# One 512-column product for the high weight part in the feed-forwards of a two-block transformer

## The chip, the cores and the metric

The kernel runs on one core of a Trainium2 chip. The metric is the device time of one execution in microseconds (us). Before the change it is 1501.49 us, the median of three runs (1499.78 to 1502.46).

The engines are named as in the profile: PE (TensorE, matrix products), PEld (its weight loads), DVE (VectorE), ACT (ScalarE), POOL (GpSimd) and SP (SyncE, which issues the DMAs here).

## The reference

The input is 256 tokens of 1024 features. A first transformer block has sliding-window and differential attention, then cross attention, then a feed-forward. A second part follows with two layers; each has a feed-forward, a mixer (convolution with latent attention in layer 0, sparse attention in layer 1) and another feed-forward. Nine modulation rows per layer come from a product of a vector `c` with a wide matrix. The parts that the change touches:

```python
u = rms_norm(x, g_mlp[l]) @ w_up[l]                  # first block, 1024 -> 4096
x = x + jnp.square(jax.nn.relu(u)) @ w_down[l]

def swiglu(h, w13, w2):                              # second part, 1024 -> 2 x 2816
    a, b = jnp.split(h @ w13, 2, axis=-1)
    return (jax.nn.silu(a) * b) @ w2

mod = c_act @ ada_w[l] + ada_b[l]                    # nine rows of 1024
h = modulate(x, norm_g[l, 0], sh1, sc1)
x = x + 0.5 * g1[:, None] * swiglu(h, ff_w13[l, 0], ff_w2[l, 0])
```

## The kernel before, in words

Activations lie transposed: features on the 128 partitions, the 256 tokens along the free axis. Every float32 operand of a weight product is used in two parts, a rounded high part and the rest as a low part, and a product is the sum of three: high weight by high activation, high weight by low activation, low weight by high activation (`mm3`). Each of the three takes a 128x128 weight tile as the stationary operand and streams 256 columns.

Weights arrive by DMA in units of 1 MB (16 tiles) into four buffers `raw`. For each half unit (8 tiles, called a split) ACT copies `raw` into the rounded `whi`, and DVE forms `wlo` as `raw` minus `whi` (line 404). `pump` keeps these splits up to three steps of 8 tiles ahead of the products; the low part is issued one split behind the high part.

The order on every engine is the order in which the Python code issues it; there is no scheduler. `run` walks a list of steps. For a step of 8 tiles it first calls `pump`, then issues what was deferred (the splitting of a feed-forward's results into `gh` and `gl`), then the products, and if these end a pair of column tiles, the code that takes the results out of PSUM (`evac`).

- `pairs` makes the steps of `w_up` (16 pairs, 8 row tiles deep) and of `w13` (four feed-forwards of 22 pairs, 8 deep). The first two or three pairs of a `w13` run before the norm is known and go another way (`head`). A pair takes 16 tiles and one PSUM tile of 512 columns, 256 for each column tile.
- `singles` makes the steps of `w_down` (8 column tiles, 32 deep) and of `w2` (8 column tiles, 22 deep). Each result is added to the residual `x` on DVE (lines 1259, 1261), and `norm_part` takes the next norm's sums.
- For `w_up` the results go through DVE (relu and scaling, line 1344) and ACT (square). For `w13`, ACT takes the silu of the first half from PSUM and DVE multiplies by the second half from PSUM (line 1398).
- `with_ada` puts the products for the modulation rows between the steps, from 98 us to about 1100 us: ACT scales a piece of `raw` by the vector and POOL adds it to a sum (line 726). Once two rows are summed, a few products on PE bring them into place.

The feed-forwards of the second part are called (layer, number): (0,0), (0,1), (1,0), (1,1). Their matrices are `w13_00` to `w13_11` and `w2_00` to `w2_11`. Products are all issued at line 345 and activations at line 318, which are helpers.

Of the kernel before, what the change touches and what calls it, by code (L numbers as in the profile page):

```python
# [41 lines left out]
GP = 64  # L42
# [32 lines left out]
def pack_cols(w):  # L75
    """column tiles one after the other, k inside"""
# [4 lines left out]
def early_order(K, M):  # L81
    """(column tile, row tile) in turn: the first half of the rows for the first half of the columns comes first"""
# [12 lines left out]
def pack_rows(w, kk):  # L95
    """kk row tiles a unit, all columns of each"""
# [5 lines left out]
def pack_ada(w):  # L102
    """for each modulation row, units of two row tiles"""
# [154 lines left out]
def merge(a, b):  # L258
    """two lists of steps, each in its order, spread evenly over one another"""
# [11 lines left out]
def rounds(n, *stages, lags=(0, 1, 3, 5)):  # L271
    """the stages of n items, each stage so many rounds behind the first; later stages first in a round"""
# [9 lines left out]
class Kernel:  # L282
    def __init__(self, tc, ctx, dram, out):
# [18 lines left out]
    def t(self, name, shape=None, dt=F):  # L302
        """short-lived"""
# [16 lines left out]
    def table(self, func):  # L320
        """loads the table of a function ahead of its use"""
# [4 lines left out]
    def copy(self, out, in_):  # L326
        """PSUM -> SBUF on whichever of the two engines had less"""
# [11 lines left out]

    def split(self, hi, lo, src):  # L340
# [6 lines left out]
    def mm3(self, out, w, x, start, stop, swap=False):  # L347
        """float32 product of operands in two parts; w stationary unless swap"""
        (wh, wl), (xh, xl) = w, x
        prod = [(wh, xh), (wh, xl), (wl, xh)]  # L350
        if swap:
            prod = [(xh, wh), (xh, wl), (xl, wh)]
        for n, (l, r) in enumerate(prod):
# [59 lines left out]
    def second(self):  # L413
        """the low part of the last split, one split behind its high part"""
# [35 lines left out]
    # ---- products with weights  # L450
    def pairs(self, name, x, kc, evac, unit0=0, npairs=None, st=None, head=0, tags=("mm", "mm"),
              biased=None):
        """steps: column tiles in pairs, k outside; evac(pair, psum [P, 2, S]); the first head pairs are of
        activations not yet normed (their norm's state in st), with the shift in two columns behind them"""
# [23 lines left out]
        for s0 in range(0, total, sub_tiles):  # L478
            def fn(hi, lo, s0=s0):
                for t in range(s0, min(s0 + sub_tiles, total)):  # L480
# [4 lines left out]
                    xh, xl = x[0](k), x[1](k)  # L485
                    fl = dict(start=k == 0, stop=k == kc - 1)
                    if pr < head:
# [3 lines left out]
                        xs = self.h[0][:, k, :]  # L491
# [1335 lines left out]
```

## Time and profile before

| what | value |
|---|---|
| median of three runs | 1501.49 us |
| span of the profiled execution, from the first to the last instruction | 1497.7 us |
| median less span (what lies around it) | 3.8 us |
| mean granted TensorE clock | 0.994 |
| PE busy | 1454.4 us, 97% |
| DVE busy | 1056.4 us, 71% |
| ACT busy | 918.8 us, 61% |
| POOL busy | 635.8 us, 42% |
| DMA moved | 312 MB, 208 GB/s on average |

The profile has no time of its own for the profiled execution besides the span. Products overlap in the records (each is shown for some 280 ns while a new one starts every 120 ns), so a busy PE is read by the distance between starts and not by the length of one product. The other three engines start an operation some 0.1 us before the one before it has ended; here too the distance between starts is what counts.

### The profile page before, as it was taken

The page shows a single profiled execution, that of the slowest core. Times are in us where ns is not written, and L with a number is a line of the kernel's source. Part 1 is how long each engine was busy: PE and PEld are TensorE (multiplying, and loading weights), DVE is VectorE, ACT ScalarE, POOL GpSimd, SP SyncE. Part 2 cuts the span into 40 slices and gives each one's busy share as a digit, 9 for nine tenths or more (in the row PEclk, how much of TensorE's full clock was granted, in tenths as well). Part 3 has the DMA queues.
Part 4 walks back from the last instruction along what each step waited for, and adds up shares of the span by engine and source line. Part 5 has one row for each costly group of instructions (what it writes and reads, how often), then busy time and mean ns, then how long its engine had stood idle before and what let it go on. Part 6 is the DMA issues. An engine that isn't in the chain of part 4 may idle for free.

```text
span 1497.7 us, 28352 instructions
## 1 busy us (share of the span) xinstructions
PE 1454.4 (97%) x11478; PEld 1384.8 (92%) x11478; DVE 1056.4 (71%) x1643; ACT 918.8 (61%) x1666; POOL 635.8 (42%) x466
## 2 busy tenths in 40 slices
PE   8998999999999999998999999999999999999997
PEld 8887989999989989997899999899999877999997
DVE  7967767776658777679887676677665777764553
ACT  6546766777657567664677666576654555654442
POOL 3102433545874567753546659466553200500021
PEclk9999999999999999999999999999999999999999
DMA  8344646677665777654548777577754510355551
GB/s 316 117 141 165 211 159 226 245 268 277 250 253 194 292 255 272 253 195 165 182 172 289 275 277 259 204 274 279 288 215 175 197 57 5 137 197 183 184 174 51
DMA packets 46067, 312.00 MB, mean 208 GB/s; under 512 B 5232, under 2 KB 7024, under 8 KB 9072
## 3 DMA queue, kind: packets, MB, share of 16 engines
q1 hardware_dynamic: 45936, 310.19, 57.7%
q8 instruction: 90, 1.47, 0.4%
q14 instruction: 41, 0.34, 0.1%
HBM read 309.12 MB, written 1.05 MB: 207 GB/s over the span
## 4 chain that ended last, share of the span: by engine, by line
PE 69%; DVE 15%; ACT 7%; DMA 5%; issue 3%; POOL 2%; SPq 0%; POOLq 0%; ACTq 0%; DVEq 0%
PE mm L345 59%; DVE wlo L404 5%; DMA raw<-w 3%; PE o L345 3%; PE sc L345 2%; ACT whi L318 2%; POOL adacc L726 2%; ACT raw L318 1%; PE mmt L345 1%; DVE hlo L653 1%; PE pT L845 1%; DVE hlo L563 1%; PE ada L345 1%; DVE gl L342 1%; DMA raw<-w_up 1%
## 5 line engine op out<-in xcount | busy, mean ns | idle before, releaser
L404 DVE TENSOR_TENSOR wlo<-raw,whi 128x1024 fp32r<-128x1024 f32 (+2 forms) x438 | 625.5, 1434 | 51.0 <-ACT whi L318 50.4
L726 POOL TENSOR_TENSOR adacc<-adacc,raw 128x512 f32<-128x512 f32 x252 | 431.9, 1739 | 415.5 <-ACT raw L318 338.8
L345 PE MATMUL mm<-hlo,whi 128*128 128x256 f32 x1960 | 556.8, 284 | 4.5 <-DVE hlo L653 4.1
L345 PE MATMUL mm<-hhi,whi 128*128 128x256 f32 (+1 forms) x1960 | 558.4, 285 | 1.1 <-ACT whi L318 1.1
L345 PE MATMUL mm<-hhi,wlo 128*128 128x256 f32 (+1 forms) x1960 | 553.4, 282 | 4.6 <-DVE wlo L404 4.6
L318 ACT ACTIVATE whi<-raw 128x1024 fp32r<-128x1024 f32 (+2 forms) x438 | 453.1, 1044 | 112.6 <-DMA raw<-w 75.3
L345 PEld LDWEIGHTS mm<-hlo,whi 128*128 128x128 f32 x1960 | 370.1, 189 | 8.3 <-DVE hlo L653 5.6
L345 PEld LDWEIGHTS mm<-hhi,wlo 128*128 128x128 f32 x1960 | 371.2, 189 | 7.0 <-DVE wlo L404 6.6
L345 PEld LDWEIGHTS mm<-hhi,whi 128*128 128x128 f32 x1960 | 370.3, 189 | 5.1 <-issue 2.5
L345 PE MATMUL mm<-gh,whi 128*128 128x256 f32 x960 | 272.6, 284 | 0.0
L345 PE MATMUL mm<-gh,wlo 128*128 128x256 f32 x960 | 271.6, 283 | 0.0
L345 PE MATMUL mm<-gl,whi 128*128 128x256 f32 x960 | 271.6, 283 | 0.0
L345 PEld LDWEIGHTS mm<-gh,whi 128*128 128x128 f32 x960 | 184.2, 192 | 4.3 <-issue 3.4
L345 PEld LDWEIGHTS mm<-gl,whi 128*128 128x128 f32 x960 | 184.2, 192 | 0.0
L345 PEld LDWEIGHTS mm<-gh,wlo 128*128 128x128 f32 x960 | 184.2, 192 | 0.0
L318 ACT ACTIVATE raw<-raw,sc 128x512 f32<-128x512 f32 x252 | 166.9, 711 | 0.6 <-DMA raw<-ada 0.5
L1398 DVE TENSOR_TENSOR ft<-mm,ft 128x256 f32<-128x256 f32 x79 | 33.4, 423 | 111.6 <-ACT ft L318 111.4
L342 DVE TENSOR_TENSOR gl<-ft,gh 128x256 fp32r<-128x256 f32 x120 | 74.1, 628 | 46.0 <-ACT gh L318 45.8
L569 POOL TENSOR_SCALAR xg<-x,M 128x256 f32<-128x256 f32 x40 | 58.3, 1458 | 98.6 <-DVE x L1261 92.3
L318 ACT ACTIVATE p<-sc,nm 128x128 f32<-128x128 f32 (+1 forms) x120 | 49.9, 421 | 74.1 <-DVE r L829 29.4
L318 ACT ACTIVATE ft<-mm 128x256 f32<-128x256 f32 x79 | 29.8, 378 | 93.5 <-PE mm L345 93.5
L585 POOL TENSOR_TENSOR acc<-acc,sq 128x256 f32<-128x256 f32 x60 | 60.4, 1009 | 44.1 <-ACT sq L318 37.1
(298 smaller groups left out, 1908.4 us busy)
## 6 DMA issues: line engine op xcount, KB each, us to landing
raw<-w SPq DMA_DIRECT2D x132, 1024.0 KB, 4.9
raw<-ada SPq DMA_DIRECT2D x72, 1024.0 KB, 6.2
raw<-w_up SPq DMA_DIRECT2D x16, 1024.0 KB, 5.0
raw<-w_down SPq DMA_DIRECT2D x16, 1024.0 KB, 5.4
raw<-hy_in SPq DMA_DIRECT2D x8, 1024.0 KB, 4.9
raw<-w_in SPq DMA_DIRECT2D x6, 1024.0 KB, 8.0
raw<-nsa_in SPq DMA_DIRECT2D x6, 1024.0 KB, 4.9
raw<-w_ck SPq DMA_DIRECT2D x4, 1024.0 KB, 4.8
```

The costliest lines, as they stand in the source:

```text
L318: return self.nc.scalar.activation(out, in_, func, **k)
L342: self.nc.vector.tensor_tensor(lo, src, hi.bitcast(F), OP.subtract)
L345: self.nc.tensor.matmul(out, lhsT, rhs, start=start, stop=stop, skip_group_check=True)
L404: self.behind = lambda hi=hi[:, :b - a], lo=lo[:, :b - a], src=src: self.nc.vector.tensor_tensor(lo, src, hi.bitcast(F), OP.subtract)
L563: self.deferred.append(lambda: nc.vector.scalar_tensor_tensor(lo, xc, gain(c), hi.bitcast(F), op0=OP.mult, op1=OP.subtract))
L569: nc.gpsimd.tensor_scalar(st["xg", c], xc, gain(c), None, op0=OP.mult)
L585: nc.gpsimd.tensor_tensor(acc, st["acc" + key], sq, OP.add)
L653: nc.vector.scalar_tensor_tensor(*last, op0=OP.add, op1=OP.subtract)
L726: nc.gpsimd.tensor_tensor(half, half, src, OP.add)
L845: self.nc.tensor.transpose(ps[:, s, :], src, self.eye)
L1398: nc.vector.tensor_mul(s, ps[:, 1, :], s)
```

## The change

In `w_up`, `w_down`, `w13` (without its first pairs) and `w2`, a tile's product is issued by the new `mm2`: one product of the high weight part with both parts of the activations, which lie side by side in 512 columns, into a whole PSUM tile of 512 columns; then one product of the low weight part with the high activations, added to the half that holds high by high. The two halves are added when the result leaves PSUM. For `w_up` and `w13` the new `summed` does it: ACT copies the first half to SBUF, DVE adds the second half to it; the silu, the multiplication and the relu then read SBUF. For `w_down` and `w2` the residual is updated twice. A pair of column tiles now takes two PSUM tiles (tags `mm` and `T`) in place of one; the modulation rows' products move from tag `T` to tag `O`. So that both parts lie side by side, `h` becomes one tile of low, high and two shift columns, and the buffers of pool `gp` are made in pairs: 32 of 512 columns in place of 64 of 256. All other products keep three products per tile. The removal of comments is left out below.

```diff
-GP = 64
+GP = 32
...
+    def summed(self, ps):
+        t = self.t("ft")
+        self.act(t, ps[:, 0, :])
+        self.nc.vector.tensor_add(t, ps[:, 1, :], t)
+        return t
...
+    def mm2(self, out, w, x, start, stop):
+        (wh, wl), (xh, _, both) = w, x[:3]
+        self.mm(out.rearrange("p a b -> p (a b)"), wh, both, start=start, stop=False)
+        self.mm(out[:, self.hi_at(x), :], wl, xh, start=False, stop=stop)
...
@@ pairs
-                        if r == 0:
+                        if r == 0 and wide:
+                            state["ps"] = [self.ps("mm", [P, 2, S], "mm"), self.ps("mm", [P, 2, S], "T")]
+                        elif r == 0:
                             state["ps"] = self.ps("mm", [P, 2, S], tags[pr % 2])
-                        self.mm3(state["ps"][:, m, :], w, (xh, xl), start=r == 0, stop=k == kc - 1)
+                        if wide:
+                            self.mm2(state["ps"][m], w, x(k), start=k == 0, stop=k == kc - 1)
+                        else:
+                            self.mm3w(state["ps"][:, m, :], w, (xh, xl), start=r == 0, stop=k == kc - 1)
@@ singles
-                            state[m] = self.ps("mm", [P, S], "S" if early else "mm")
+                            state[m] = self.ps("mm", [P, S], "S") if early else self.ps("mm", [P, 2, S], "mm")
...
+                    if early:
+                        self.mm3w(state[m], w, x(k)[:2], start=first, stop=k == kc - 1)
+                    else:
+                        self.mm2(state[m], w, x(k), start=first, stop=k == kc - 1)
@@ h_part
+        return self.h[:, c, S:2 * S], self.h[:, c, :S], self.h[:, c, :2 * S], None
@@ rows, post of the modulation rows
-                ps = self.ps("ada", [P, 512], "T")
+                ps = self.ps("ada", [P, 512], "O")
...
-                tp = self.ps("adat", [P, 4, P], "T")
+                tp = self.ps("adat", [P, 4, P], "O")
@@ residual
-                if gate is None:
-                    nc.vector.tensor_add(xc, ps, xc)
-                else:
-                    nc.vector.scalar_tensor_tensor(xc, ps, gate(m), xc, op0=OP.mult, op1=OP.add)
+                for part in (ps,) if len(ps.shape) == 2 else (ps[:, 0, :], ps[:, 1, :]):
+                    if gate is None:
+                        nc.vector.tensor_add(xc, part, xc)
+                    else:
+                        nc.vector.scalar_tensor_tensor(xc, part, gate(m), xc, op0=OP.mult, op1=OP.add)
@@ evac_up
-                t = self.t("ft")
-                nc.vector.scalar_tensor_tensor(t, ps[:, m, :], 0.0, stu["rbs"], op0=OP.max, op1=OP.mult)
+                t = self.summed(ps[m])
+                nc.vector.scalar_tensor_tensor(t, t, 0.0, stu["rbs"], op0=OP.max, op1=OP.mult)
                 self.act(t, t, AF.Square)
@@ ff, evac
-                self.act(s, ps[:, 0, :], AF.Silu)
-                nc.vector.tensor_mul(s, ps[:, 1, :], s)
+                s = self.summed(ps[0])
+                self.act(s, s, AF.Silu)
+                nc.vector.tensor_mul(s, self.summed(ps[1]), s)
```

On DVE, in `w13_10`, from one pair of column tiles to the next, before the change. `ft` is the result on its way out of PSUM (`mm`), `gl` its low part, `wlo` the low part of a split.

```order
L1398 TENSOR_TENSOR ft_11949<-mm_11897,ft_11949 128x256
L404 TENSOR_TENSOR wlo_11923<-raw_11656,whi_11922 128x1024
L342 TENSOR_TENSOR gl_11953<-ft_11949,gh_11952 128x256
L404 TENSOR_TENSOR wlo_11955<-raw_11656,whi_11954 128x1024
L1398 TENSOR_TENSOR ft_12018<-mm_11962,ft_12018 128x256
```

The same stretch after the change (`gg` now holds both parts of a result).

```order
L365 TENSOR_TENSOR ft_10637<-mm_10596,ft_10637 128x256
L365 TENSOR_TENSOR ft_10641<-mm_10597,ft_10641 128x256
L1450 TENSOR_TENSOR ft_10637<-ft_10641,ft_10637 128x256
L444 TENSOR_TENSOR wlo_10618<-raw_10432,whi_10617 128x1024
L370 TENSOR_TENSOR gg_10645<-ft_10637,gg_10645 128x256
L444 TENSOR_TENSOR wlo_10653<-raw_10432,whi_10652 128x1024
L365 TENSOR_TENSOR ft_10698<-mm_10660,ft_10698 128x256
```

Where one multiplication from PSUM stood, there are now two additions from PSUM and a multiplication that reads two SBUF tiles.

On ACT, in the same stretch, before the change (`raw` times `sc` is a piece of the modulation rows).

```order
L318 ACTIVATE ft_12018<-mm_11962 128x256
L318 ACTIVATE raw_11697<-raw_11697,sc_707 128x512 x2
L318 ACTIVATE whi_12029<-raw_11785 128x1024
L318 ACTIVATE gh_12021<-ft_12018 128x256
L318 ACTIVATE whi_12062<-raw_11879 128x1024
```

After.

```order
L339 ACTIVATE ft_10637<-mm_10596 128x256
L339 ACTIVATE ft_10637<-ft_10637 128x256
L339 ACTIVATE ft_10641<-mm_10597 128x256
L339 ACTIVATE raw_10346<-raw_10346,sc_683 128x512 x2
L339 ACTIVATE whi_10652<-raw_10432 128x1024
L339 ACTIVATE gg_10645<-ft_10637 128x256
L339 ACTIVATE whi_10678<-raw_10526 128x1024
```

The silu no longer reads PSUM but waits for DVE's first addition, and the second copy out of PSUM stands behind it, ahead of the pieces of the modulation rows and of the next split.

## Rows read from the trace of the kernel before

**Rows 1.** page, first part: span, then busy time, share and instructions of each engine

```profile
span 1497.7 us, 28352 instructions
...
PE 1454.4 (97%) x11478; PEld 1384.8 (92%) x11478; DVE 1056.4 (71%) x1643; ACT 918.8 (61%) x1666; POOL 635.8 (42%) x466
```

**Rows 2.** page, chain that ended last, by engine

```profile
PE 69%; DVE 15%; ACT 7%; DMA 5%; issue 3%; POOL 2%; SPq 0%; POOLq 0%; ACTq 0%; DVEq 0%
```

**Rows 3.** stretches: us, each engine's busy us (instructions), PE clock, DMA share, GB/s

```profile
252.00:346.00 94.00, 92.28 (x754) 88.60 (x753) 69.04 (x99) 70.16 (x128) 42.60 (x28) 1.00 0.71 252
346.00:440.00 94.00, 92.84 (x759) 90.21 (x758) 59.93 (x58) 60.64 (x91) 72.89 (x47) 1.00 0.74 276
480.00:572.00 92.00, 89.74 (x728) 86.47 (x727) 68.35 (x70) 60.47 (x97) 54.48 (x30) 1.00 0.75 272
781.50:842.00 60.50, 60.50 (x509) 60.50 (x508) 42.69 (x43) 43.77 (x70) 39.15 (x22) 1.00 0.79 283
979.00:1076.00 97.00, 97.00 (x812) 96.03 (x812) 69.48 (x72) 68.22 (x109) 59.38 (x33) 1.00 0.78 286
1318.00:1430.00 112.00, 112.00 (x940) 112.00 (x939) 61.92 (x82) 52.88 (x82) 0.00 (x0) 1.00 0.55 189
```

**Rows 4.** waits of PE: us in total, times, longest

```profile
PE mm L345 <- DVE wlo L404: 4.6, 9, 0.9
```

**Rows 5.** timeline of DVE, one pair of w13_11, nothing on POOL

```profile
1385.24 0.42 DVE L1398 TENSOR_TENSOR ft<-mm,ft 128x256 f32<-128x256 f32 x1 [2.71 <-ACT ft L318]
1385.58 1.22 DVE L404 TENSOR_TENSOR wlo<-raw,whi 128x1024 fp32r<-128x1024 f32 x1
1386.71 0.42 DVE L342 TENSOR_TENSOR gl<-ft,gh 128x256 fp32r<-128x256 f32 x1
1387.05 1.22 DVE L404 TENSOR_TENSOR wlo<-raw,whi 128x1024 fp32r<-128x1024 f32 x1
1390.97 0.42 DVE L1398 TENSOR_TENSOR ft<-mm,ft 128x256 f32<-128x256 f32 x1 [2.71 <-ACT ft L318]
```

**Rows 6.** timeline of ACT, the same pair

```profile
1384.82 0.38 ACT L318 ACTIVATE ft<-mm 128x256 f32<-128x256 f32 x1 [3.15 <-PE mm L345]
1385.10 1.05 ACT L318 ACTIVATE whi<-raw 128x1024 fp32r<-128x1024 f32 x1
```

**Rows 7.** pieces of the chain in order: start, us, what

```profile
1312.96 167.39 PE mm L345 x1397
```

**Rows 8.** timeline of PE, 512-column products of w_in_v

```profile
68.99 0.39 PE L345 MATMUL mm<-whi,hlo 128*128 128x512 f32 x1
...
71.09 0.40 PE L345 MATMUL mm<-whi,hlo 128*128 128x512 f32 x1
```

**Rows 9.** timeline of DVE, results of w_up leaving PSUM

```profile
259.07 0.76 DVE L1344 SCALAR_TENSOR_TENSOR ft<-mm,rbs 128x256 f32<-128x256 f32 x2 [2.09 <-PE mm L345]
```

**Rows 10.** timeline of ACT, their squares

```profile
259.52 0.75 ACT L318 ACTIVATE ft<-ft 128x256 f32<-128x256 f32 x2 [1.94 <-DVE ft L1344]
```

**Rows 11.** timeline of DVE, an operation and the next on its result

```profile
720.01 0.42 DVE L1439 TENSOR_TENSOR cvv<-mm,cu 128x256 f32<-128x256 f32 x1 [0.60 <-PE mm L345]
720.47 1.46 DVE L1444 TENSOR_SCALAR ca<-cvv,colp 128x256 f32<-128x256 f32 x1
```

**Rows 12.** DVE line 342: count, shortest, median and longest ns

```profile
L342 DVE TENSOR_TENSOR gl<-ft,gh x120: 410/425/1511, 255.1 to 1426.8; 128x256 fp32r<-128x256 f32 x120
```

**Rows 13.** DVE line 404, the same

```profile
L404 DVE TENSOR_TENSOR wlo<-raw,whi x438: 686/1218/2366, 7.8 to 1480.8; 128x1024 fp32r<-128x1024 f32 x144, 128x608 fp32r<-128x608 f32 x2
```

**Rows 14.** DVE line 1398, the same

```profile
L1398 DVE TENSOR_TENSOR ft<-mm,ft x79: 409/425/428, 470.5 to 1425.4; 128x256 f32<-128x256 f32 x79
```

**Rows 15.** POOL line 726, the same

```profile
L726 POOL TENSOR_TENSOR adacc<-adacc,raw x252: 1266/1499/2354, 124.5 to 1097.5; 128x512 f32<-128x512 f32 x126
```

**Rows 16.** timeline of PE, the last sum of squares

```profile
1489.35 0.61 PE L345 MATMUL ssum<-ones,sq 128*128 128x1 f32 x4 [0.75 <-ACT sq L318]
```

**Rows 17.** groups of ACT: count, busy us, mean ns, idle before and releaser

```profile
L318 ACT ACTIVATE whi<-raw 128x1024 fp32r<-128x1024 f32 x431 | 448.6, 1050 | 112.6 <-DMA raw<-w 75.3 <-DMA raw<-w_down 15.8 <-PE mm L345 8.3
```

More of the change, by code (lines that the diff above doesn't have):

```diff
@@ L292, in __init__, with two @@
         self.flip, self.now = 0, None
+        self.half = {}
         self.deferred, self.behind = [], None
     def g(self, name, dt=F, shape=None):
-        return self.gp.tile(shape or [P, S], dt, name=name, tag="g")
+        key = (name if name in PAIRED else "", dt)
+        t = self.half.pop(key, None)
+        n = 1
+        if t is None:
+            n = 0
+            t = self.half[key] = self.gp.tile([P, 2, S], dt, name=name, tag="g")
+        ap = t[:, n, :]
+        if shape:
+            names = " ".join(f"d{i}" for i in range(len(shape) - 1))
+            ap = ap.rearrange(f"p ({names}) -> p {names}", **{f"d{i}": x for i, x in enumerate(shape[1:])})
+        return ap
+    def two(self, name):
+        if name == "gg":
+            self.half.clear()
+        t = self.gp.tile([P, 2, S], R, name=name, tag="g")
+        return t[:, 0, :], t[:, 1, :], t.rearrange("p a b -> p (a b)")
     def w(self, name, shape, dt=F, tag=None, bufs=2):
@@ L345, in mm, with mm3, mm3w, hi_at @@
         self.nc.tensor.matmul(out, lhsT, rhs, start=start, stop=stop, skip_group_check=True)
-    def mm3(self, out, w, x, start, stop, swap=False):
+    def mm3(self, out, w, x, start, stop):
         (wh, wl), (xh, xl) = w, x
[L350 to L353, printed above, removed]
+        for n, (l, r) in enumerate([(xh, wh), (xh, wl), (xl, wh)]):
             self.mm(out, l, r, start=start and n == 0, stop=stop and n == 2)
+    def mm3w(self, out, w, x, start, stop):
+        (wh, wl), (xh, xl) = w, x
+        for n, (l, r) in enumerate([(wh, xh), (wh, xl), (wl, xh)]):
+            self.mm(out, l, r, start=start and n == 0, stop=stop and n == 2)
+    def mm2(self, out, w, x, start, stop):
+        (wh, wl), (xh, _, both) = w, x[:3]
+        self.mm(out.rearrange("p a b -> p (a b)"), wh, both, start=start, stop=False)
+        self.mm(out[:, self.hi_at(x), :], wl, xh, start=False, stop=stop)
+    def hi_at(self, x):
+        return 1 if len(x) > 3 else 0
     def stream_init(self, steps):
@@ L451, in pairs @@
     def pairs(self, name, x, kc, evac, unit0=0, npairs=None, st=None, head=0, tags=("mm", "mm"),
-              biased=None):
+              biased=None, wide=False):
         steps, state = [], {}
@@ L692, in dst, with h_part @@
             if c == 0:
-                hi = self.work.tile([P, KD, S + 2], R, name="hhi", tag="hhi", bufs=1)
-                lo = self.work.tile([P, KD, S], R, name="hlo", tag="hlo", bufs=1)
-                self.h = (hi, lo)
-            return self.h[0][:, c, :S], self.h[1][:, c, :]
-        return dst
+                self.h = self.work.tile([P, KD, 2 * S + 2], R, name="h", tag="h", bufs=1)
+            return self.h_part(c)
+        return dst
+    def h_part(self, c):
+        return self.h[:, c, S:2 * S], self.h[:, c, :S], self.h[:, c, :2 * S], None
     def h_src(self):
-        return (lambda k: self.h[0][:, k, :S], lambda k: self.h[1][:, k, :])
+        return self.h_part
     def ada_steps(self, l):
@@ L810, in softmax @@
         if roomy:
[L811 removed]
+            p = self.g("p0")[:, :P], self.g("p0")
         else:
@@ L885, in split_out @@
     def split_out(self, ps, name, scale=None):
-        hi, lo = self.g(name + "h", R), self.g(name + "l", R)
+        pair = self.two(name)
+        hi, lo = pair[:2]
         if scale is None:
@@ L891, in split_out @@
             self.nc.vector.scalar_tensor_tensor(lo, ps, scale, hi.bitcast(F), op0=OP.mult, op1=OP.subtract)
-        return hi, lo
+        return pair
     def zeroed(self, name, keep):
@@ L951, in late_loads @@
         nc.sync.dma_start(self.posi[1], self.dram["pos"][:, 1, :])
-        self.mem = [self.g(f"mem{c}") for c in range(KD)]
+        self.mem = [self.g("mem") for c in range(KD)]
         for c in range(KD):
@@ L1053, in mdst @@
         def mdst(c):
-            hm[c] = (self.g(f"hmh{c}", R), self.g(f"hml{c}", R))
+            hm[c] = self.two("hm")
             return hm[c]
@@ L1342, in evac_up @@
             for m in range(2):
-                t = self.t("ft")
-                nc.vector.scalar_tensor_tensor(t, ps[:, m, :], 0.0, stu["rbs"], op0=OP.max, op1=OP.mult)
+                t = self.summed(ps[m])
+                nc.vector.scalar_tensor_tensor(t, t, 0.0, stu["rbs"], op0=OP.max, op1=OP.mult)
                 self.act(t, t, AF.Square)
-                gh, gl = self.g("gh", R), self.g("gl", R)
-                self.deferred.append(lambda gh=gh, gl=gl, t=t: self.split(gh, gl, t))
-                gg[2 * pr + m] = (gh, gl)
-        gsrc = (lambda k: gg[k][0], lambda k: gg[k][1])
+                g = gg[2 * pr + m] = self.two("gg")
+                self.deferred.append(lambda g=g, t=t: self.split(g[0], g[1], t))
+        gsrc = lambda k: gg[k]
         self.gg, self.gsrc = gg, gsrc
-        mlp = self.pairs("w_up", h, KD, evac_up, npairs=16, st=stu)
+        mlp = self.pairs("w_up", h, KD, evac_up, npairs=16, st=stu, wide=True)
         M = self.M[0]
@@ L1448, in evac_z @@
                         nc.vector.tensor_mul(a, src, a)
-                        hi, lo = self.g("yh", R), self.g("yl", R)
-                        self.split(hi, lo, a)
-                        y[c] = (hi, lo)
+                        y[c] = self.two("y")
+                        self.split(y[c][0], y[c][1], a)
         scale = 96 ** -0.5
```

51 lines of the change are left out of this document (25 added, 26 removed).

## The prediction

> **What bounds the kernel now.** I read the busy shares first. PE is busy 97% of the span, DVE 71%, ACT 61% [rows 1]. PE leads the chain of waits too, but only with 69%; DVE has 15% [rows 2]. In all, products wait only 4.6 us for low weight parts, in nine waits [rows 4]. So PE sets the pace, with DVE close behind it in places.
>
> Where, the stretches show [rows 3]. A pair of `w_up` or `w13` takes 16 tiles, 48 products before. I divide a stretch's PE instructions by 48 (a few products for modulation rows make the pair count slightly too high) and get, per pair, time and busy DVE:
>
> - `w_up` (252 to 346): 15.7 pairs, 5.99 us, DVE 4.40.
> - `w13_00` (480 to 572): 15.2 pairs, 6.07 us, DVE 4.51.
> - `w13_01` (781.5 to 842): 10.6 pairs, 5.71 us, DVE 4.03.
> - `w13_10` (979 to 1076): 16.9 pairs, 5.73 us, DVE 4.11.
> - `w13_11` (1318 to 1430): 19.6 pairs, 5.72 us, DVE 3.16.
>
> The last has nothing on POOL, and PE clock is 1.00 (2.4 GHz) in all of them. DVE's extra microsecond in the others comes from POOL. The low weight part takes 1.22 us at the median and up to 2.37 [rows 13], the low part of a result 0.43 and up to 1.51 [rows 12]; both read two SBUF tiles. The multiplication from PSUM never leaves 0.41 to 0.43 [rows 14]. POOL's addition goes the same way, 1.27 to 2.35 us [rows 15].
>
> **The products.** The change takes 2,480 products away: `w_up` 256 tiles, `w_down` 256, `w2` 4 x 176, `w13` 4 x 352 less the 144 tiles of the first nine pairs, one product for each tile. The step of a 256-column product comes from a pair without disturbance: DVE's operations after it start at 1385.24 and 1390.97, 5.73 us or 48 x 119.4 ns [rows 5]; 1,397 products of the last stretch give 119.8 [rows 7]. For 512 columns the trace has the products of `w_in_v`: starts at 68.99 and 71.09, nine steps, 233.3 ns [rows 8]. There the weights stream and the activations are stationary, the other way round than in the new product; I take the same step. A tile falls from 358.2 to 233.3 + 119.4 = 352.7 ns, 5.5 ns less (6.1 by 119.8). All 2,480 tiles together are worth 13.6 us (15.1), and that is the most PE alone can give. A pair goes from 5.73 to 5.64 us.
>
> The Trainium skill (TensorE: Matmul & The Clock Gate, Back-to-back issue gap) gives 131 ns as the sustained spacing of 512-column products in streams with weight loads; by it a tile would save 108 ns. The row above, 233 ns, speaks against it. It is the last rival.
>
> **What leaving PSUM costs.** The change adds 190 copies on ACT (32 in `w_up`, 2 x 79 in `w13`), 190 additions on DVE, and 40 residual updates. They stand in the evacuation of a pair, between the splits that feed PE; behind them on DVE wait the low weight parts, and PE waits for those. For a pair of `w13` I follow DVE from start to start:
>
> - First addition to second: the first result must reach ACT, 0.45 us (259.07 to 259.52) [rows 9, 10]; the silu gives way to the copy after 0.28 (as a copy to a split, 1384.82 to 1385.10 [rows 6]) to 0.37 (half of two squares, 0.75 [rows 10]), I take 0.34; the copy is followed by DVE after 0.42 (1384.82 to 1385.24) [rows 5, 6]. Sum 1.21. DVE stands still for most of it, since nothing else is queued there.
> - Second addition to the multiplication on its result: 0.46 (720.01 to 720.47) [rows 11].
> - Multiplication to the next: 0.34 (1385.24 to 1385.58) [rows 5]. It reads two SBUF tiles now. Beside POOL its like goes from 0.43 up to 1.51 [rows 12]; the extra lies between 0 and, since half of these rows show none, half of 1.1; I take 0.2, towards the median. With the 59 multiplications beside POOL and the 32 rescalings below, the ends move the sum by -18 and +32 us.
>
> That is 2.01 us without POOL and 2.21 with, where before the one multiplication took 0.34: 1.67 and 1.87 more. The other POOL delays I leave as they are, since POOL's work does not change.
>
> On the multiplication, the Trainium skill (SBUF — State Buffer, Who interferes with whom) says that a DVE instruction with two SBUF inputs is shut out by a GpSimd instruction that reads SBUF, while one with a single SBUF input is not. The trace agrees: 428 ns at most from PSUM, 1,511 ns from SBUF. By its full block each of the 91 could wait a whole POOL addition, 1.3 us, and the sum would be some 100 us higher; the median row says that most do not wait at all.
>
> For `w_up`: first addition, rescaling 0.46 later, square 0.45, copy 0.34, second addition 0.42, rescaling 0.46, next 0.34; sum 2.47, with 0.2 for each of two rescalings that now read SBUF 2.87. Before: twice 0.34. So 2.19 more.
>
> DVE then needs, per pair: `w_up` 6.59 us, `w13_00` 6.38, `w13_01` 5.90, `w13_10` 5.98, `w13_11` 4.83. Only the last is below PE's 5.64. In the other four PE must follow DVE.
>
> ACT gets the two short copies, and waits for DVE's addition; its load per pair (68.22 us over 16.9 pairs in `w13_10`, 4.04 us [rows 3]) plus 0.34 and that 0.45 stays below 5.
>
> **The sum**, against the pairs' own times before:
>
> - `w_up` 16 x (6.59 - 5.99) = +9.6
> - `w13_00` 19 x (6.38 - 6.07) = +5.9
> - `w13_01` 20 x (5.90 - 5.71) = +3.8
> - `w13_10` 20 x (5.98 - 5.73) = +5.0
> - `w13_11` 20 x (5.64 - 5.73) = -1.8
> - `w_down` and `w2`: 960 x 5.5 ns = -5.3; DVE has room there for the one more update a column tile (59.93 of 94 us busy in `w_down` [rows 3]).
> - The end: the last residual takes one more update, 0.46, which the last sum of squares waits for (PE already idles 0.75 there [rows 16]); the same at five earlier ends, mostly under the next first pairs: +1.0 in all.
> - Credit for the splits that run ahead: after a pair's end DVE needs about 0.42 + 2.2 + 1.6 us to the next low part that PE lacks, and PE has two more steps, 5.64 us, so each of the four stretches may fall 1.4 us behind at no cost: -5.6.
>
> Total +12.6 us. Span 1497.7 becomes 1510.3; with the 3.8 us between span and median, 1514 us. The measured pair times of DVE vary, so the likeliest case's own range is 1504.5 to 1524.
>
> The modulation rows' move to another PSUM tag, the pairing of buffers and the new layout of `h` I cost at nothing: POOL, SP and the loads keep their order, and the tags have the same number of buffers. Without that cover it is a wait of a few hundred ns at a modulation row or in an attention stage.
>
> **Rivals.**
>
> 1. *The gain of PE comes through* (0.24). DVE's cycle stays under 5.64 us in the busy stretches. For `w13_01` this needs 0.26 us less than I count, for `w13_10` 0.34, and it is a matter of POOL: while DVE stands still between the two additions, POOL can work undisturbed, so part of the microsecond that POOL costs DVE per pair may go. The single point is whether that pays back 0.3 us a pair. Against it: DVE already idles more than a microsecond per pair before, in which POOL had the same freedom. If so, 13.6 less 1.0 for the end: 1489 us.
> 2. *DVE without reserve delays the loads* (0.13). ACT waits 75.3 us in all for `raw` [rows 17], with DMA 71 to 79% busy in these stretches [rows 3]. A buffer is freed by the low part on DVE; a later DVE means a later load, and nothing is left for catching up. Then no credit for running ahead (+5.6), and both middle feed-forwards at the load of `w13_00`, 0.4 us a pair more for 40 pairs (+16): 1535 us.
> 3. *Both sides cancel* (0.11): extra on DVE of only 0.2 us a pair less over 75 pairs, about -12: 1502 us.
> 4. *The wide product is much cheaper than in the row* (0.02). If it took no longer than a narrow one, 119.4 ns, PE would need 3.8 us a pair and DVE would set every pair: +24 in the four stretches, -18 in `w13_11` (4.83), up to -115 in `w_down` and `w2`, +1 at the end: 1394 us. The 512-column rows speak against it.
>
> The Trainium skill's spacing, named above, points to this rival.
>
> That the change does not act as told is excluded: the program has the 2,480 products fewer.
>
> **Numbers.** The forecast has 0.50: 1514 us. Changes below 0.2% (3 us) can't be told from none. Slower by more: the forecast but for its lowest edge (0.47) and rival 2, 0.60. Faster: rivals 1 and 4, 0.26. Within: 0.14. The range reaches from rival 1 to rival 2, 1490 to 1535.
>
> **What would show it.** After the change: `w13_11` near 5.64 us a pair with DVE idle before its first addition; in the other four stretches PE waits for `wlo`, far above 4.6 us in total, pairs of 5.9 us and more, and ACT waiting for DVE's additions. A 512-column step near 233 ns confirms the PE term. If `w13_01` and `w13_10` also run at 5.64 with PE idle nowhere, the DVE sum is wrong and rival 1 holds; if ACT waits much more than 75 us for loads, rival 2.

## The result, and the profile after

The changed kernel takes 1573.34 us (1572.28 to 1575.48, four runs) where the one before, on the same chip, takes 1500.65. The ratio is 1.0481, 95% interval 1.0463 to 1.0499. Slower was forecast, but by 12.6 us; the profiled spans differ by 1571.7 - 1497.7 = 74.0 us, far above the range.

The page of the changed kernel, against [rows 1, 2]: span, busy time of each engine, and the chain that ended last.

```profile
span 1571.7 us, 23765 instructions
...
PE 1465.5 (93%) x8998; PEld 1261.8 (80%) x8998; DVE 1174.8 (75%) x1873; ACT 982.9 (63%) x1856; POOL 631.7 (40%) x466
...
PE 31%; DVE 20%; ACT 7%; DMA 5%; issue 2%; POOL 1%; POOLq 0%; ACTq 0%; SPq 0%; DVEq 0%
```

PE has 2,480 instructions fewer; DVE has more to do. The shares of the chain after the change add up to 66% only, since the profile could follow it back no further than to 521.9 us. Of the part that it has, PE holds 31 of 66, less than half, where before it held 69% of the whole; DVE holds 20 of 66, where it had 15%. The waits of PE for low weight parts and for POOL's sums of the modulation rows (us, times, longest), the first against [rows 4]:

```profile
PE mm L373 <- DVE wlo L444: 53.2, 53, 2.7
PE ada L373 <- POOL adacc L776: 14.6, 13, 2.7
```

PE waited 4.2 us for POOL's sums before. For the stages, two sets of windows, each from the first split of a result to the last one of a stage behind its `head` pairs. Columns as in [rows 3]. First before, 14, 18, 19, 19 and 19 pairs of `w_up`, `w13_00`, `w13_01`, `w13_10`, `w13_11`:

```profile
255.08:341.06 85.98, 84.62 (x704) 83.27 (x697) 62.21 (x89) 65.73 (x119) 40.24 (x27) 1.00 0.72 254
472.40:581.47 109.07, 106.81 (x870) 103.54 (x870) 81.30 (x85) 72.32 (x116) 64.20 (x35) 1.00 0.73 267
778.65:889.95 111.30, 110.93 (x918) 108.83 (x917) 79.15 (x82) 76.91 (x123) 68.11 (x37) 1.00 0.77 277
978.12:1088.07 109.95, 109.95 (x921) 108.97 (x920) 77.69 (x82) 76.93 (x122) 66.51 (x37) 1.00 0.78 285
1319.94:1426.84 106.90, 106.90 (x898) 106.90 (x897) 57.52 (x77) 49.18 (x77) 0.00 (x0) 1.00 0.57 195
```

The same pairs after the change:

```profile
257.47:369.72 112.25, 90.74 (x468) 74.28 (x467) 77.55 (x117) 74.53 (x147) 40.06 (x28) 0.95 0.54 197
503.80:625.13 121.33, 109.83 (x591) 91.63 (x589) 97.42 (x121) 84.79 (x153) 62.97 (x36) 0.97 0.64 237
825.05:950.87 125.82, 114.17 (x622) 94.04 (x621) 102.72 (x121) 89.54 (x161) 66.92 (x38) 1.00 0.66 244
1043.65:1166.60 122.95, 112.74 (x622) 93.96 (x620) 102.66 (x121) 88.66 (x160) 66.96 (x38) 1.00 0.68 250
1398.92:1503.39 104.47, 104.47 (x597) 91.43 (x597) 73.50 (x115) 64.28 (x115) 0.00 (x0) 1.00 0.54 193
```

Dividing by the pairs gives us per pair:

| stage | time before | after | forecast | DVE busy before | after |
|---|---|---|---|---|---|
| w_up | 6.14 | 8.02 | 6.59 | 4.44 | 5.54 |
| w13_00 | 6.06 | 6.74 | 6.38 | 4.52 | 5.41 |
| w13_01 | 5.86 | 6.62 | 5.90 | 4.17 | 5.41 |
| w13_10 | 5.79 | 6.47 | 5.98 | 4.09 | 5.40 |
| w13_11 | 5.63 | 5.50 | 5.64 | 3.03 | 3.87 |

Only the last stage, which has nothing on POOL, gets faster. Its two times are some 2% too short, since the first pairs of its windows leave PSUM late and so close together: after them DVE's multiplications start 5.73 us apart before [rows 5] and 5.62 after the change. The chain's last piece of PE, mostly that stage and `w2_11` (start, us, what; against [rows 7]):

```profile
1390.31 163.27 PE mm L373 x932
```

932 products are 466 tiles, 350 ns each, where 352.7 was forecast; 16 of them are 5.61 us, where 5.64 was. DVE leaving PSUM there, against [rows 5] (start, us, line, operation, idle before):

```profile
1400.39 0.42 DVE L365 TENSOR_TENSOR ft<-mm,ft 128x256 f32<-128x256 f32 x1
1401.56 0.42 DVE L365 TENSOR_TENSOR ft<-mm,ft 128x256 f32<-128x256 f32 x1 [0.76 <-ACT ft L339]
1402.02 0.42 DVE L1450 TENSOR_TENSOR ft<-ft 128x256 f32<-128x256 f32 x1
1402.36 1.22 DVE L444 TENSOR_TENSOR wlo<-raw,whi 128x1024 fp32r<-128x1024 f32 x1
```

Addition to addition 1.17 us, then 0.46 and 0.34: the 2.01 us of the forecast are 1.97. So both terms of the sum come out, within 2%, where POOL is silent. Beside POOL, in one of the longest pairs of `w13_10`, DVE runs

```profile
1064.77 0.41 DVE L365 TENSOR_TENSOR ft<-mm,ft 128x256 f32<-128x256 f32 x1
1065.94 0.43 DVE L365 TENSOR_TENSOR ft<-mm,ft 128x256 f32<-128x256 f32 x1 [0.76 <-ACT ft L339]
1066.40 0.42 DVE L1450 TENSOR_TENSOR ft<-ft 128x256 f32<-128x256 f32 x1
1066.74 2.32 DVE L444 TENSOR_TENSOR wlo<-raw,whi 128x1024 fp32r<-128x1024 f32 x1
1068.99 1.51 DVE L370 TENSOR_TENSOR gg<-ft,gg 128x256 fp32r<-128x256 f32 x1
1070.42 2.31 DVE L444 TENSOR_TENSOR wlo<-raw,whi 128x1024 fp32r<-128x1024 f32 x1
1072.66 0.41 DVE L365 TENSOR_TENSOR ft<-mm,ft 128x256 f32<-128x256 f32 x1
```

while POOL has this (the same view):

```profile
1066.65 7.23 POOL L776 TENSOR_TENSOR adacc<-adacc,raw 128x512 f32<-128x512 f32 x4 [3.22 <-issue]
```

From addition to addition 7.9 us, where the stage's mean is 6.47: both low weight parts take 2.3 us for 1.2, the low part of the result 1.5 for 0.4, but additions and multiplication are as short as ever. In `w_up` ACT shows where the time goes:

```profile
306.60 0.36 ACT L339 ACTIVATE ft<-mm 128x256 f32<-128x256 f32 x1
308.86 0.42 ACT L339 ACTIVATE ft<-ft 128x256 f32<-128x256 f32 x1 [1.90 <-DVE ft L1396]
309.18 0.37 ACT L339 ACTIVATE ft<-mm 128x256 f32<-128x256 f32 x1
310.50 0.42 ACT L339 ACTIVATE ft<-ft 128x256 f32<-128x256 f32 x1 [0.95 <-DVE ft L1396]
```

```profile
306.99 0.42 DVE L365 TENSOR_TENSOR ft<-mm,ft 128x256 f32<-128x256 f32 x1 [0.85 <-ACT ft L339]
307.45 1.38 DVE L1396 SCALAR_TENSOR_TENSOR ft<-ft,rbs 128x256 f32<-128x256 f32 x1
309.58 0.42 DVE L365 TENSOR_TENSOR ft<-mm,ft 128x256 f32<-128x256 f32 x1 [0.76 <-ACT ft L339]
310.04 0.42 DVE L1396 SCALAR_TENSOR_TENSOR ft<-ft,rbs 128x256 f32<-128x256 f32 x1
```

ACT copies, stands until DVE has added and rescaled, squares, and does the same again. All in all, in the window of `w_up` above:

```profile
ACT ft L339 <- DVE ft L1396: 37.7, 28, 2.3
```

74.53 us busy and 37.7 of waiting are 112.2 of the window's 112.25 us. ACT does nothing but work and wait for DVE. In `w13_10` it is much the same, 88.66 us busy and the waits below, 121.2 of 122.95 us. There ACT waits for the first addition, which stands in DVE's queue behind the stretched low parts:

```profile
ACT ft L339 <- DVE ft L365: 25.0, 19, 2.4
ACT whi L339 <- DMA raw<-w: 7.5, 6, 2.3
```

### The profile page after: what moved, and what is told of

Its sections match the earlier page's. It is cut to its first block, busy times and chain, and to the rows that moved or that the text cites. A ratio compares the mean times of both kernels' runs of the same rounds, so it can differ in the third digit from the quotient of the medians.

```text
span 1571.7 us, 23765 instructions
## 1 busy us (share of the span) xinstructions
PE 1465.5 (93%) x8998; PEld 1261.8 (80%) x8998; DVE 1174.8 (75%) x1873; ACT 982.9 (63%) x1856; POOL 631.7 (40%) x466
## 4 chain that ended last, share of the span: by engine, by line
PE 31%; DVE 20%; ACT 7%; DMA 5%; issue 2%; POOL 1%; POOLq 0%; ACTq 0%; SPq 0%; DVEq 0%
PE mm L373 25%; DVE wlo L444 10%; DMA raw<-w 5%; DVE gg L370 3%; ACT ft L339 2%; ACT whi L339 2%; PE o L373 2%; DVE ft L365 2%; PE sc L373 2%; POOL adacc L776 1%; DVE h L701 1%; ACT raw L339 1%; DVE ft L1450 1%; PE mmt L373 1%; PE pT L895 1%
## 5 line engine op out<-in xcount | busy, mean ns | idle before, releaser
L373 PE MATMUL mm<-h,whi 128*128 128x512 f32 (+2 forms) x2400 | 718.2, 360 | 5.8 <-DVE h L701 4.4
L776 POOL TENSOR_TENSOR adacc<-adacc,raw 128x512 f32<-128x512 f32 x252 | 428.7, 1725 | 491.8 <-ACT raw L339 369.2
L373 PE MATMUL mm<-h,wlo 128*128 128x256 f32 (+1 forms) x1960 | 562.0, 287 | 49.7 <-DVE wlo L444 49.5
L373 PEld LDWEIGHTS mm<-h,whi 128*128 128x128 f32 x2400 | 429.0, 191 | 79.2 <-DVE h L701 8.2
L373 PEld LDWEIGHTS mm<-h,wlo 128*128 128x128 f32 x1960 | 374.2, 191 | 67.8 <-DVE wlo L444 66.5
L373 PE MATMUL mm<-gg,whi 128*128 128x512 f32 x960 | 341.7, 400 | 1.3 <-ACT whi L339 1.3
L373 PE MATMUL mm<-gg,wlo 128*128 128x256 f32 x960 | 270.7, 282 | 3.8 <-DVE wlo L444 3.7
L373 PEld LDWEIGHTS mm<-gg,whi 128*128 128x128 f32 x960 | 181.7, 189 | 50.2 <-issue 4.7
L373 PEld LDWEIGHTS mm<-gg,wlo 128*128 128x128 f32 x960 | 182.7, 190 | 5.9 <-DVE wlo L444 5.9
L370 DVE TENSOR_TENSOR gg<-ft,gg 128x256 fp32r<-128x256 f32 x120 | 88.1, 745 | 21.3 <-ACT gg L339 21.1
L373 PE MATMUL mm<-o,whi 128*128 128x256 f32 x448 | 83.4, 287 | 1.3 <-DVE x L1311 1.2
L633 POOL TENSOR_TENSOR acc<-acc,sq 128x256 f32<-128x256 f32 x60 | 59.4, 993 | 44.6 <-ACT sq L339 41.9
```

What stands on the lines that cost most here:

```text
L370: self.nc.vector.tensor_tensor(lo, src, hi.bitcast(F), OP.subtract)
L373: self.nc.tensor.matmul(out, lhsT, rhs, start=start, stop=stop, skip_group_check=True)
L633: nc.gpsimd.tensor_tensor(acc, st["acc" + key], sq, OP.add)
L776: nc.gpsimd.tensor_tensor(half, half, src, OP.add)
```

## The experiments

My first theory was that ACT and DVE, which each take their work in order, wait for one another in turn inside the evacuation. The rival was that POOL slows DVE's reads of two SBUF tiles. Further rivals were the wide product or the new layout itself, and loaded buffers that POOL holds too long. All kernels start from the changed one, if not said otherwise. Each ratio is to the kernel before, measured beside the experiment; its medians there are 1499.4 to 1500.3 us. Of long lines the diffs show the ends.

**One: the wide product in `w_down` and `w2` alone.**

```diff
-npairs=16, st=stu, wide=True)
+npairs=16, st=stu)
-biased=evac, wide=True)
+biased=evac)
```

(and the evacuation of before for these pairs)

> The changed kernel, but w_up and w13 keep three products of 256 columns and the evacuation of before; only w_down and w2 (960 column-by-row tiles) take the wide product. Theory (the loss sits in the evacuation of the pairs): 960 x 5.5 ns less than before, 1495 us, pair times of w_up and w13 as before (6.1, 6.0, 5.8, 5.7, 5.6 us). Rival (the new layout of h, the tags of PSUM or the paired buffers cost something): well above 1505 us, with the pairs themselves slower.

1499.08 us, ratio 0.9993 (0.9975 to 1.0012). Layout, tags and buffers cost nothing that can be seen. But the 5 us did not come either. From the first to the last residual update, on DVE's timeline, `w2_00`, `w2_10` and `w2_11` take 1.4, 1.7 and 2.1 us less than before, `w_down` 0.2 and `w2_01` 0.9 more. In these two PE waits longer for POOL's sums of the modulation rows, 2.8 us for 1.2 in `w_down` and 2.9 for 1.2 in `w2_01`, which is most of what is missing there; no run takes this wait away by itself.

**Two: the same instructions, copies first.**

```diff
-s = self.summed(ps[0])
-self.act(s, s, AF.Silu)
-nc.vector.tensor_mul(s, self.summed(ps[1]), s)
+s, s1 = self.sums(ps)
+self.act(s, s, AF.Silu)
+nc.vector.tensor_mul(s, s1, s)
...
+def sums(self, ps):
+    ts = [self.t("ft") for _ in range(2)]
+    for m in range(2):
+        self.act(ts[m], ps[m][:, 0, :])
+    for m in range(2):
+        self.nc.vector.tensor_add(ts[m], ps[m][:, 1, :], ts[m])
+    return ts
```

> The changed kernel with the same instructions in another order at the evacuation of a pair: both copies on ACT first, then both additions on DVE, then the rest (w13: silu, multiplication; w_up: two rescalings, two squares). Theory (ACT and DVE wait for one another in turn inside the evacuation, and what is queued behind waits too): two of the four hand-offs go, DVE's chain of a w13 pair falls from 2.0 to about 1.25 us, and more than half of the 73 us comes back, 1510 to 1540 us. Rival (POOL slows DVE's reads of two SBUF tiles, whatever their order): no instruction is less and POOL is as before, 1560 us or more.

1532.32 us, ratio 1.0222 (1.0203 to 1.0241): 41 of the 73 us come back, as the theory had it. In `w_up` the theory is also right about the way: 96.72/14 = 6.91 us a pair for 8.02, and ACT waits 21.0 us for DVE's rescalings where it waited 37.7. In the `w13` it is not. The window of `w13_10`, 19 pairs, and the group of the low parts of the results in the whole kernel (count | busy us, mean ns | idle before):

```profile
1005.91:1121.23 115.32, 111.09 (x616) 93.28 (x616) 92.59 (x121) 89.10 (x160) 64.55 (x37) 1.00 0.71 268
```

```profile
L378 DVE TENSOR_TENSOR gg<-ft,gg 128x256 fp32r<-128x256 f32 x120 | 67.9, 576 | 48.2 <-ACT gg L339 48.1
```

DVE's idle time per pair hardly changes, (115.32 - 92.59)/19 = 1.20 us for 1.07. Its busy time falls from 5.40 to 4.87: the low parts of the results take 576 ns in the mean where the changed kernel has 745, and in this window the low weight parts take 1610 for 1723. The order has changed what POOL hits.

**Three: the gain of PE without the addition.**

```diff
-s = self.summed(ps[0])
-self.act(s, s, AF.Silu)
-nc.vector.tensor_mul(s, self.summed(ps[1]), s)
+self.act(s, ps[0][:, 0, :], AF.Silu)
+nc.vector.tensor_mul(s, ps[1][:, 0, :], s)
```

(`w_up` likewise)

> The changed kernel with the copy and the addition left out in the evacuation of w_up and w13: silu, multiplication and rescaling read the first half alone, so a part of the product is missing from the result. All products are as changed. Theory (evacuation alone makes the loss): the gain of PE stands by itself, 1500.6 - 13.6 = 1487 us, 1484 to 1492. Rival (wide products, layout or tags bring waits of their own): above 1500 us.

1489.75 us, ratio 0.9931 (0.9914 to 0.9948). The wide products by themselves gain 10 us, where 13.6 was expected; the loss comes in with the evacuation.

**Four and five: POOL's additions cut, after and before.**

```diff
-nc.gpsimd.tensor_tensor(half, half, src, OP.add)
+nc.gpsimd.tensor_tensor(half[:, :8], half[:, :8], src[:, :8], OP.add)
```

> The changed kernel with POOL's additions for the modulation rows cut from 512 columns to 8; ACT's scaling, the loads and all waits stay (the modulation is wrong then). Theory of the hand-offs between ACT and DVE: they are there without POOL too; the loss falls only by what POOL stretches DVE, a third or so, 1535 to 1555 us. Rival, POOL's contention: the four slow stretches run like w13_11, about 5.5 us a pair, and the time is 1485 to 1500 us.

> The kernel before with POOL's additions for the modulation rows cut from 512 columns to 8, as in e4 (the modulation is wrong then): the other half of e4. If POOL's slowing of DVE is the whole reason of the loss, the change without it is worth its PE gain, and this one is 1480.7 + 13 = 1490 to 1497 us. If w_up loses by its hand-offs between ACT and DVE without POOL too (in e4 its pair still took 7.34 us, 6.14 before the change, some 19 us over 16 pairs), this one is faster than e4: w13 at 5.63 us a pair, w_up about 6, 1455 to 1478 us.

After: 1480.71 us, ratio to before 0.9876 (0.9861 to 0.989). Before: 1472.79 us, 0.9815 (0.9798 to 0.9831). My first theory falls for `w13` as it stood: the hand-offs are all still there, and the three stages run at 5.6 to 5.8 us a pair. But what they cost ACT has fallen, from 25.0 us in `w13_10` to this:

```profile
ACT ft L339 <- DVE ft L365: 10.1, 19, 0.7
```

The groups of low weight parts and low parts of results, first in the changed kernel, then with POOL cut:

```profile
L444 DVE TENSOR_TENSOR wlo<-raw,whi 128x1024 fp32r<-128x1024 f32 x431 | 622.3, 1450 | 45.9 <-ACT whi L339 45.4
L370 DVE TENSOR_TENSOR gg<-ft,gg 128x256 fp32r<-128x256 f32 x120 | 88.1, 745 | 21.3 <-ACT gg L339 21.1
...
L1450 DVE TENSOR_TENSOR ft<-ft 128x256 f32<-128x256 f32 x79 | 33.6, 425 | 2.7
```

```profile
L444 DVE TENSOR_TENSOR wlo<-raw,whi 128x1024 fp32r<-128x1024 f32 x431 | 532.5, 1241 | 43.0 <-ACT whi L339 42.2
...
L370 DVE TENSOR_TENSOR gg<-ft,gg 128x256 fp32r<-128x256 f32 x120 | 51.9, 444 | 33.6 <-ACT gg L339 33.3
```

90 and 36 us less on DVE, in the same instructions. (The cut also takes away 13.9 of the 14.6 us that PE waits for POOL's sums, and the granted clock is 0.996 for 0.986, so not all that it gives back is DVE's.) But `w_up` does not recover. The windows of `w_up` and `w13_10` with POOL cut, and ACT's waits in the first:

```profile
250.34:353.04 102.70, 88.03 (x471) 70.85 (x469) 66.26 (x117) 74.57 (x147) 9.77 (x28) 1.00 0.58 215
...
968.00:1074.66 106.66, 106.66 (x612) 92.53 (x612) 75.09 (x121) 88.84 (x160) 20.37 (x38) 1.00 0.77 288
```

```profile
ACT ft L339 <- DVE ft L1396: 28.1, 28, 1.2
```

102.70/14 = 7.34 us a pair, and 74.57 + 28.1 us of ACT fill it. The kernel before, with POOL cut, needs 82.57/14 = 5.90 there:

```profile
249.67:332.24 82.57, 82.57 (x694) 81.84 (x687) 53.42 (x89) 66.52 (x119) 9.75 (x28) 1.00 0.75 268
```

So the two kinds of stage differ: the `w13` lose only with POOL's additions, while `w_up` loses most of it without them too (7.34 us a pair for 5.90; with them it is 8.02 for 6.14).

**Six: POOL works as long, but holds no buffer.**

```diff
-nc.gpsimd.tensor_tensor(half, half, src, OP.add)
+v = half.rearrange("p (a b) -> p a b", a=32)
+nc.gpsimd.tensor_tensor(v, v, self.Z[:, None, 16:32].to_broadcast([P, 32, 16]), OP.add)
```

> The changed kernel in which POOL's additions for the modulation rows keep their 512 columns but take the second operand from a constant tile of zeros instead of the loaded one (the modulation is wrong then). A loaded buffer is free after ACT's scaling and no longer waits for POOL, while POOL reads and writes SBUF as long as before. Theory (POOL slows DVE's reads of two SBUF tiles): DVE's low parts stay at about 1.45 us, the time stays near the changed kernel's, 1555 to 1580 us. Rival (POOL holds the loaded buffers, so the loads come late): as e4, 1480 to 1500 us.

1588.64 us (1586.82 to 1589.33), ratio 1.0589 (1.0573 to 1.0605). The loads come sooner (ACT waits 16.2 us for those of `w`, where it waits 49.0 in the changed kernel), and nothing is gained, so POOL's hold on the buffers is not the reason. The low weight parts stay at 1449 ns:

```profile
L444 DVE TENSOR_TENSOR wlo<-raw,whi 128x1024 fp32r<-128x1024 f32 x431 | 621.7, 1449 | 30.1 <-ACT whi L339 29.6
...
L1451 DVE TENSOR_TENSOR ft<-ft 128x256 f32<-128x256 f32 x79 | 49.2, 623 | 2.7
```

That it is 15 us slower than the changed kernel was not expected. The multiplication now is hit too (623 ns for 425, 16 us over 79), and the mean granted clock is 0.973 where the changed kernel has 0.986; no run separates the two.

**Seven: silu, squares, multiplication and splits issued later.**

```diff
+s, s1 = self.sums(ps)              # both copies, then both additions
+def last():
+    nc.vector.tensor_mul(s, s1, s)
+    self.split(g[0], g[1], s)
+def silu():
+    self.act(s, s, AF.Silu)
+    self.deferred.append(last)     # one step of 8 tiles later
+self.deferred.append(silu)
```

(`w_up`: the squares one step later, the splits another)

> The changed kernel with the same instructions, but no engine is made to wait for the other inside the evacuation: both copies, both additions (and rescalings); the silu or the squares are issued a step of eight tiles later, multiplication and split another step later. POOL as it is. Theory (what is lost is DVE's stretched work plus its idle time in hand-offs, 0.8 to 1.0 us a w13 pair, and in w_up ACT's waits for DVE): the idle goes and DVE's 5.1 to 5.4 us a pair (as in e2) fit beside PE's 5.5, w_up falls below 6.3; 1488 to 1508 us. Rival (DVE's stretched work alone sets the pace; hand-offs only fill time that was free): as e2 or above, 1525 us and more.

1526.35 us, ratio 1.018 (1.0162 to 1.0198). This is the number of the rival. `w_up` falls to 91.15/14 = 6.51 us, nearly as the theory had it, but `w13` stays at 6.3 to 6.5. The multiplication, moved to another moment, is now what POOL hits:

```profile
L1464 DVE TENSOR_TENSOR ft<-ft 128x256 f32<-128x256 f32 x79 | 79.9, 1011 | 0.0
```

1011 ns for 425, with the same operands. The waits are not all gone in the `w13`, contrary to the plan: ACT's split of the result is issued right behind that multiplication, and ACT now waits for it instead, in `w13_10` (999.24 to 1120.04 us) nearly as long as it waited for additions before:

```profile
ACT gg L339 <- DVE ft L1464: 20.9, 15, 3.0
```

So this run does not tell DVE's stretched work from the waits that it causes.

**Eight: seven with POOL cut.** The two edits together.

> e9 and e4 together: nobody waits inside the evacuation, and POOL's additions for the modulation rows are cut to 8 columns (the modulation is wrong then). It is to be held against e5 (before, with POOL cut: 1472.8 us) and e4 (changed, with POOL cut: 1480.7 us). Theory (two causes: hand-offs in w_up, POOL's slowing of DVE in the three busy w13): with both away the gain of PE comes through, w_up 5.6 to 5.9 us a pair, w13 5.5 to 5.65, 1456 to 1466 us. Rival (w_up is slow by the added work itself on ACT and DVE, not by its order): w_up stays at 7 us a pair or more, 1474 us and above.

1454.04 us, ratio 0.97 (0.9679 to 0.972). `w_up` and `w13_10`:

```profile
251.35:330.29 78.94, 78.94 (x453) 69.24 (x452) 62.95 (x118) 73.38 (x145) 16.89 (x28) 1.00 0.75 281
...
941.60:1048.62 107.02, 107.02 (x615) 92.94 (x614) 73.26 (x120) 88.68 (x159) 19.15 (x38) 1.00 0.78 290
```

78.94/14 = 5.64 and 107.02/19 = 5.63 us a pair, PE busy throughout. The change is then worth 1472.79 - 1454.04 = 18.8 us. Not all of it is the products': the kernel before, with POOL cut, has its evacuation undeferred, and its `w_up` takes 5.90 us where 48 products need 5.73; it was not run deferred. The runs side by side, in us:

| | POOL's additions whole | cut |
|---|---|---|
| before | 1500.65 | 1472.79 |
| changed | 1573.34 | 1480.71 |
| changed, deferred | 1526.35 | 1454.04 |

POOL's additions cost the kernel before 28 us, the changed one 93, the deferred one 72. The hand-offs without POOL cost 1480.71 - 1454.04 = 26.7 us, and `w_up` by itself has as much: (102.70 - 78.94) x 16/14 = 27.

**Nine: `w_up` alone.** The wide product and its evacuation in `w_up`, all else as before.

```diff
-biased=evac, wide=True)
+biased=evac)
```

(this is for the `w13`; `singles` with three products)

> The wide product in w_up alone, with the changed evacuation; w13 and all column-by-column products (w_down, w2) as before. Theory (w_up loses by itself, 8.0 for 6.1 us a pair over 16 pairs): 1500 + 28 = 1528, 1522 to 1532 us. Rival (w_up is only slow since later stages hold back the loads, or the change's other parts carry it): below 1515 us.

1528.56 us, ratio 1.0195 (1.0174 to 1.0216): 28 to 29 of the 73 us. Its 14 pairs of `w_up` take 112.26 us, as in the changed kernel (112.25).

**Ten: the wide product only where it gains.**

```diff
-npairs=16, st=stu, wide=True)
+npairs=16, st=stu)
-biased=evac, wide=True)
+biased=evac, wide=last)
-self.residual(self.st, lambda m: M[:, s0 + 2, m:m + 1], nxt, plain=last))
+self.residual(self.st, lambda m: M[:, s0 + 2, m:m + 1], nxt, plain=last), wide=(l, f) != (0, 1))
```

(`w_down` with `wide=False`; where it is false, three products and the evacuation of before)

> The wide product only where the runs so far show a gain: w13_11 and the w2 of the feed-forwards 00, 10 and 11; w_up, w_down, w2_01 and the other w13 as before. Theory: w13_11 20 x 0.13 us and the three w2 1.4 to 2.0 us each (from e1), 1492 to 1496 us, faster than both kernels. Rival (what a stage gains is lost in waits at the next): 1498 to 1502 us.

1496.25 us (12 runs), ratio 0.9975 (0.9962 to 0.9988), at the upper edge of what was expected. It is faster than both kernels, than the one before by a quarter of a per cent, some 3 us; the interval is clear of 1, but the single runs (1492.5 to 1499.4 us) overlap with those of the kernel before (1495.6 to 1503.8).

## Why the prediction missed

The parts of the sum, in us. Measured are the pair times of the table above times all pairs of a stage, and for `w_down` and `w2` the time from the first to the last residual update.

| term | forecast | measured |
|---|---|---|
| w_up | +9.6 | +30.0 |
| w13_00, 01, 10 | +14.7 | +41.9 |
| w13_11 | -1.8 | -2.6 |
| w_down and w2 | -5.3 | +1.9 |
| ends, and credit for running ahead | -4.6 | +2.8 (the rest) |
| sum | +12.6 | +74.0 |

- **The products.** Right in kind and a little small: 351 ns a tile (5.62 us over 16) for 352.7, against 358.2 before. With copy and addition left out the kernel gains 10 us (three); deferred and with POOL cut, 19 (eight). The fourth rival falls.
- **DVE's chain in a `w13` evacuation.** Right, 1.97 us for 2.01 without POOL [rows 5, 11].
- **"ACT ... stays below 5."** This step failed, in all four slow stages. I took ACT's load from `w13_10`, 4.04 us, added one copy and one wait of 0.45, and applied it to all. In `w_up` ACT has 65.73/14 = 4.70 us of work before (and already waits 0.97 for DVE) and 5.32 after, and then waits 2.69 on top: 8.01, the whole pair. It stands still twice a pair, for an addition and a rescaling each, 0.95 us at the least and 1.90 with a rescaling that POOL has stretched to 1.38. Run eight, with the same work and no such waits, shows 5.64 us; so for `w_up` this cause is shown. In `w13_10` ACT has 4.67 us of work, waits 1.32 for DVE's addition and 0.39 for loads: 6.38 of 6.47. I had followed DVE's side of the exchange only.
- **"The other POOL delays I leave as they are, since POOL's work does not change."** This step failed too. In run four, without POOL's additions, ACT's wait in `w13_10` is 10.1/19 = 0.53 us a pair, near the 0.45 that I counted, and the `w13` run at PE's pace or close to it. With them DVE is late, and that returns twice. First, DVE is busy for longer: by what the forecast implies (the time before, 0.84 for two additions and 0.2) for 5.13, 5.21 and 5.56 us in `w13_10`, `w13_01` and `w13_00`, in fact for 5.40, 5.41 and 5.41. In the first two the splits are hit more by the same POOL work, in `w13_00` hardly. Second, DVE idles for longer, since ACT is late in turn: 1.07, 1.22 and 1.33 us a pair, where the forecast's chain has 0.83. The second part is the larger. That POOL's additions are needed for the loss in the `w13` is shown; how it divides between longer operations and the waits they bring is not.
- **Which operation is hit** depends on the moment. I charged 0.2 us to each of 91 operations. The multiplications paid nothing (425 ns), the 32 rescalings 0.16 (583 ns for 426 with POOL cut), and the low parts of the results, which I had not charged, went from 628 ns in the mean to 745; in run seven the multiplication pays 0.59. The Trainium skill (SBUF — State Buffer, Who interferes with whom) has the rule that a VectorE instruction with two SBUF inputs is shut out by a GpSimd instruction that reads SBUF. Runs four and six agree with it on what is hit.
- **The credit.** The credit of 5.6 us was not there: in the four stages PE waits 46.6 us for low weight parts (18.8, 10.3, 8.9 and 8.6). That the splits cannot run ahead once ACT always works or waits for DVE is how I read it; no run tests it.
- **`w_down` and `w2`.** That DVE has room there was assumed for all five. `w2_00`, `w2_10` and `w2_11` gain, `w_down` and `w2_01` do not (run one). PE's longer wait for POOL's sums there is most of what is missing; the cause is not tested further. In the whole kernel this wait is 14.6 us for 4.2; at most a few hundred ns at a modulation row had been counted. In the changed kernel `w2_01` also ran at a granted clock of 0.95.
- **The rivals.** The first and the third needed a DVE cycle below the count; it was above. The second, DVE without reserve, was right in its kind and had 0.13, but its mechanism was not: ACT waits less for loads than before (7.5 us in `w13_10` for 19.1, and in all 49.0 for `w` [rows 17: 75.3]), and in run six earlier free buffers bring no gain.

The clock has a share that no run isolates. Over four-us windows, the full speed that PE lacked sums to 8.5 us before and 21.5 after. Three windows of the changed kernel in `w_up` (columns as above; the clock is the third number from the end):

```profile
284.00:286.00 2.00, 0.06 (x1) 0.00 (x0) 1.90 (x3) 1.05 (x4) 0.00 (x0) 1.00 0.42 176
286.00:288.00 2.00, 1.85 (x7) 1.55 (x8) 0.18 (x2) 2.00 (x5) 1.84 (x2) 0.63 0.02 4
288.00:290.00 2.00, 2.00 (x8) 1.71 (x7) 2.00 (x3) 1.40 (x3) 0.68 (x1) 0.52 0.44 53
```

PE has stood still for 2 us, and for the next 3 or so it gets about half of its clock, 1.2 GHz for 2.4. Four other drops, near 300, 457, 532 and 993 us, also came right behind a stand of PE. A wait here costs more than its own length, but in these stages PE waits for DVE anyway, so part of that may be hidden.

## What to carry to other kernels

When an edit puts a hand-off between two in-order engines, add up both engines: busy time plus every wait of one for the other, stage by stage; the larger sum is the pace, and a stage with another load needs its own sum. An operation that POOL stretches is not a fixed price: when the work moves by a step, another instruction is hit, and an engine that was hidden behind another has paid part of that price all along without showing it (before the change DVE's low weight parts took 1445 ns in the mean, and 1241 with POOL cut). Such a delay also returns as a wait on the engine at the other end of a hand-off. A quarter of a per cent was to be had by making the change only in `w13_11`, which has nothing on POOL, and in the three `w2` where run one showed a gain.

## What the runs showed of the hardware

- DVE's subtraction on 128x1024 with two SBUF inputs takes 1241 ns in the mean with POOL's additions cut and 1450 with them, up to 2.3 us beside a POOL addition; an addition that reads PSUM and one SBUF tile takes 424 and 421 ns, untouched.
- POOL's additions on 8 columns still take 236 ns at the median and 445 in the mean (1472 and 1725 on 512), so a cut to a 64th of the columns leaves a sixth to a quarter of the time.
- A product of 512 columns after a weight load is followed by the next after 0.23 us whichever operand streams; 256 columns take half of that (0.12).
